# The low parts of the input weights made by an adding load instead of a VectorE subtraction, in a hybrid decoder step

## The chip, the cores and the metric

One core of a Trainium2 chip runs the kernel. The metric is the time of one execution on the device in microseconds (us), taken as the median of three runs; the profile is of one further execution. Engines are named as in the profile: PE is TensorE (PEld its weight loads), DVE is VectorE, ACT is ScalarE, POOL is GpSimd, SP is SyncE, which here only issues DMAs.

## What is computed

One inference step of a one-layer hybrid decoder, on a prompt of 512 tokens and 8 sample tokens, with model width 2048. A single input projection is split by columns into an mLSTM branch (4 heads of 256), a causal convolution branch (512 channels) and a sliding-window attention branch (8 query heads); their gated outputs are concatenated, multiplied by an output projection, and normalised with the residual. Cut to what matters here:

```python
h = jnp.einsum('btd,de->bte', x, w_in)            # the input projection, split by columns
...                                               # three branches, each with its gate
merged = jnp.concatenate([m_out, c_out * jax.nn.silu(cz), a_out * jax.nn.silu(az)], axis=-1)
y = jnp.einsum('bte,ed->btd', merged, w_out)
x = layer_norm(ALPHA * x + y, ln_g, ln_b)
```

Everything is float32.

## The kernel before, in words

The projections are float32 products made of three passes over parts of reduced precision. Each operand is taken apart into a high part (a rounding cast to float32r) and a low part (the operand less its high part). `mm3` (lines 209 to 212) then issues, for one 128 x 128 piece of weights, three matmuls into the same bank: line 210 takes the high weights and the high input, line 211 the **low weights** and the high input, line 212 the high weights and the low input. A transposed input of 520 columns is resident in 16 pieces (`xh`, `xl`), and is passed in two halves of 260 columns.

**The weight stream.** The list `stream` (lines 165 to 169) names all the weights in the order of their use, in tiles of 128 x 1024 float32 (512 KB). The input projection has NE = 62 column blocks of 128, called e, and each has two tiles, so tiles 0 to 123 are the input weights; tiles 124 and up belong to the output projection. `w_load` (line 180) issues a tile's load from HBM into a raw buffer `wr` on SP's queue; there are three raw buffers. `w_split` (line 187) takes the next tile from its raw buffer, takes a slot of `wh` (tag whi, 3 buffers) and of `wl` (tag wlo, 3 buffers), and calls `split` (lines 151 to 153):

```python
def split(hi, lo, raw):
    S.copy(out=hi, in_=raw)
    V.tensor_tensor(out=lo, in0=raw, in1=hi.bitcast(F32), op=ALU.subtract)
```

So ACT makes the high part (line 152) and DVE the low part (line 153), and after both the raw buffer is free for a later load.

**What sets the order.** The main loop over e (lines 994 to 1018) stands in a manual schedule for PE, DVE and ACT: these three engines run their instructions in the order of the program. POOL and SP are not in that list; the framework orders them. At the start of e, `w_split` is called for the first tile of e+1, and in its middle for the second one. The slots of that tile are those that the tile three places earlier used, and so the cast waits for PE to end with that tile. A tile is used by 16 calls of `mm3`, that is 48 matmuls on PE. After the matmuls of a half, the results are moved out of the bank (`post`, for the attention queries `post_aq`, lines 424 to 438), and `pump` lets the branches go on by some steps, each of which adds instructions to PE, ACT, DVE, and in the mLSTM and in the layer norms also to POOL: the mask addition (line 655), the product with the decay (line 686), and the power -0.5 of a variance (`rstd`, line 223). The sample attention (`att_sample`, line 526) copies queries into a padded tile with 32 small DVE instructions (line 548), which PE's line 555 reads. Before the loop come the first two column blocks with tiles 0 to 3, and the gate computation (`gates`, line 231), whose short ACT and DVE instructions run on into the loop's first 20 us.

Of the kernel before, what the change touches and what calls it, by code (L numbers as in the profile page):

```python
# [11 lines left out]
ALU = mybir.AluOpType  # L12
# [43 lines left out]
NE = len(ORDER)  # L56

TURNED = {(_i // 4, _i // 2 % 2, _i % 2): (_i - 1,) for _i in range(1, 9)}
TURNED.update({(3, 0, 1): (8, 9, 10, 11), (3, 1, 0): (12, 13, 14), (3, 1, 1): (15,)})
CONV0 = ORDER.index(("cg", 0))  # L60


# [11 lines left out]
def body(tc, ctx, A, O):  # L74
    nc = tc.nc
    V, S, G, PE, SP = nc.vector, nc.scalar, nc.gpsimd, nc.tensor, nc.sync
# [11 lines left out]
    def nm(s):  # L88
        uid[0] += 1
        return f"{s}{uid[0]}"  # L90
# [4 lines left out]
    def mid(dt=F32):  # L95
        return work.tile([P, 520], dt, tag="M", bufs=NM, name=nm("M"))
# [54 lines left out]
# [3 lines that stand above are left out]
# [3 lines left out]
    def x_tile(tag, dt=F32R):  # L157
        return res.tile([P, TT], dt, tag=tag, bufs=NK, name=nm(tag))
# [6 lines left out]
    stream = [A["w_in"][e, hf] for hf in range(2) for e in range(2)]  # L165
# [5 lines left out]
    raws, parts = {}, {}  # L171
# [8 lines left out]
    def w_load(n):  # L180
        while pos[0] < min(n, len(stream)):
            i = pos[0]
            raws[i] = wp.tile([P, 8 * P], F32, tag="wraw", bufs=NRAW, name=nm("wr"))
            SP.dma_start(out=raws[i], in_=stream[i])
            pos[0] += 1

    def w_split(n):
        while pos[1] < min(n, len(stream)):
            i = pos[1]
            w_load(i + 1)  # L190
            raw = raws.pop(i)
            if i in kept:

                if kept.index(i) < 2:
                    parts[i] = [[x_tile(t)[:, 0:512] for _ in range(2)] for t in ("xh", "xl")]
                else:
                    parts[i] = [[mid(F32R)[:, 0:512] for _ in range(2)] for _ in range(2)]
                for kk in range(2):
                    split(parts[i][0][kk], parts[i][1][kk], raw[:, kk * 512:(kk + 1) * 512])
            else:  # L200
                parts[i] = (wp.tile([P, 8 * P], F32R, tag="whi", bufs=3, name=nm("wh")),
                            wp.tile([P, 8 * P], F32R, tag="wlo", bufs=3, name=nm("wl")))
                split(*parts[i], raw)
                if i >= b2:
                    parts[i] = [[t[:, kk * 512:(kk + 1) * 512] for kk in range(2)] for t in parts[i]]
            pos[1] += 1
            w_load(i + 1 + ahead[0])
# [672 lines left out]
    for k in range(NK):  # L880
# [35 lines left out]
        if k == 5:  # L916
            w_split(3)
        if k == 8:
            w_split(4)
# [5 lines left out]
    for e in range(2):  # L925
        for k in range(NK - TAIL, NK):
            first(e, k)
        for hf in range(2):
            (post_ak, post_av)[e](ps01[e][hf], hf)
        w_split(5 + e)  # L930
# [17 lines left out]
    def before(name, i):  # L948

        if name == "mv" and i == 2:  # L950
            drain("att")
        elif name == "mq" and i == 6:
            drain(("m", 0))
        elif name == "cg" and i == 0:
            conv_state()
        elif name in ("mz", "mo"):
            drain(("m", i // 2))
        elif name == "cz":
            drain("conv")
# [33 lines left out]
    with tc.manual_schedule(engines=MAN):  # L993
        for e in range(2, NE):
            name, i = ORDER[e]
            w_split(2 * e + 3)
            budget = BUDGET if e < CONV0 else BUDGET2
            before(name, i)
# [295 lines left out]
```

## Time and profile before

| | |
|---|---|
| median of 3 runs | 1019.48 us (1019.22 to 1019.91) |
| the profiled execution | 1019.64 us |
| its span, first to last instruction | 1017.9 us |
| TensorE clock granted, mean over the span | 0.994 of full speed |
| PE busy | 997.0 us, 98% |
| DVE busy | 657.9 us, 65% |
| ACT busy | 396.6 us, 39% |
| POOL busy | 79.8 us, 8% |
| DMA | 147.11 MB, mean 145 GB/s |

How to read it: the profiled execution's time is 1.7 us above its span, and 0.16 us above the median of the runs. Issuing DMAs and waiting on semaphores are not counted as busy. PE's busy time is the union of overlapping matmuls, so that a share near 100% says that PE is seldom left without a matmul, and not that it runs at its peak.

### The profile page before, as it was taken

What the parts mean: (1) busy time and instruction counts of PE and PEld (TensorE: products, weight loads), DVE (VectorE), ACT (ScalarE), POOL (GpSimd) and SP (SyncE); (2) the same over time, 40 slices, a digit from 0 to 9 for tenths busy, and PEclk for the clock granted to TensorE, in tenths of its full rate; (3) what the DMA queues carried; (4) which work ended last, traced back from release to release, by engine and by line L of the source; (5) the groups of instructions that cost most, each with busy time, mean ns of one, the idle gap of its engine ahead of it and who ended that gap; (6) DMA issues with size and microseconds to landing.
All of it is one profiled execution on the core that took longest, in us unless ns stands there. A gap on an engine that the chain in (4) does not pass through costs nothing.

```text
span 1017.9 us, 19338 instructions
## 1 busy us (share of the span) xinstructions
PE 997.0 (98%) x7922; PEld 975.1 (96%) x7922; DVE 657.9 (65%) x1336; ACT 396.6 (39%) x713; POOL 79.8 (8%) x88
## 2 busy tenths in 40 slices
PE   8999999999999999999999999999999999999895
PEld 8999999899999999999999999999999999998675
DVE  4654667676646746756667777878654545559855
ACT  5553455234334433434442222222243433336341
POOL 1000000010101100001000000000000000005704
PEclk9999999999999999999999999999999999999998
DMA  8332213365445436635543232323234565555852
GB/s 275 130 105 76 71 63 106 120 211 189 135 166 183 153 117 211 190 106 169 180 153 103 100 93 101 88 89 104 96 120 141 186 228 173 175 171 189 264 169 83
DMA packets 64992, 147.11 MB, mean 145 GB/s; under 512 B 16181, under 2 KB 21261, under 8 KB 64904
## 3 DMA queue, kind: packets, MB, share of 16 engines
q1 hardware_dynamic: 64056, 143.64, 43.4%
q0 software_dynamic: 848, 2.25, 0.7%
q8 instruction: 62, 1.02, 0.4%
q14 instruction: 26, 0.21, 0.1%
HBM read 130.30 MB, written 15.56 MB: 143 GB/s over the span
## 4 chain that ended last, share of the span: by engine, by line
PE 86%; DVE 5%; DMA 4%; ACT 2%; issue 2%; POOL 0%; SPq 0%; DVEq 0%; ACTq 0%; POOLq 0%
PE mm L212 26%; PE mm L210 26%; PE mm L211 26%; DMA wr<-in_w_in 2%; DMA wr<-in_w_out 2%; PE bg L210 2%; PE bg L211 2%; PE bg L212 1%; DVE wl L153 1%; PE bg L677 1%; ACT wh L152 1%; PE bg L875 1%; PE bg L1077 1%; DMA S<-in_n 0%; DVE M L1047 0%
## 5 line engine op out<-in xcount | busy, mean ns | idle before, releaser
L210 PE MATMUL mm<-xh,wh 128*128 128x260 f32 (+1 forms) x2096 | 598.0, 285 | 2.8 <-ACT wh L152 1.6
L211 PE MATMUL mm<-xh,wl 128*128 128x260 f32 (+1 forms) x2096 | 592.3, 283 | 0.0
L212 PE MATMUL mm<-xl,wh 128*128 128x260 f32 (+1 forms) x2096 | 592.3, 283 | 0.0
L210 PEld LDWEIGHTS mm<-xh,wh 128*128 128x128 f32 x2096 | 396.0, 189 | 4.2 <-ACT wh L152 1.9
L211 PEld LDWEIGHTS mm<-xh,wl 128*128 128x128 f32 x2096 | 395.3, 189 | 0.6 <-DVE wl L153 0.2
L212 PEld LDWEIGHTS mm<-xl,wh 128*128 128x128 f32 x2096 | 394.6, 188 | 0.0
L153 DVE TENSOR_TENSOR wl<-wr,wh 128x1024 fp32r<-128x1024 f32 (+2 forms) x191 | 228.2, 1196 | 129.3 <-ACT wh L152 125.9
L152 ACT CAST wh<-wr 128x1024 fp32r<-128x1024 f32 (+2 forms) x191 | 193.9, 1016 | 220.8 <-PE mm L212 143.1
L341 DVE SCALAR_TENSOR_TENSOR L<-L,cst 128x512 f32<-128x512 f32 x120 | 90.0, 750 | 2.7
L811 ACT ACTIVATE S<-mm 128x260 f32<-128x260 f32 x48 | 18.7, 389 | 97.4 <-PE mm L212 97.4
L812 DVE TENSOR_TENSOR L<-L,S 128x260 f32<-128x260 f32 x48 | 20.6, 430 | 50.5 <-ACT S L811 50.5
L223 POOL TENSOR_TENSOR T<-T,mhalf 128x1 f32<-128x1 f32 (+1 forms) x26 | 16.3, 625 | 432.2 <-DVE T L221 403.9
L609 ACT ACTIVATE L<-mm 128x260 f32<-128x260 f32 x48 | 18.5, 385 | 64.7 <-PE mm L212 64.5
L784 DVE SCALAR_TENSOR_TENSOR M<-M,T,M 128x256 f32<-128x256 f32 x64 | 31.8, 496 | 10.9 <-ACT M L781 10.9
L212 PE MATMUL mm<-L,wh 128*128 128x264 f32 x128 | 36.4, 284 | 0.0
L211 PE MATMUL mm<-L,wl 128*128 128x264 f32 x128 | 36.4, 284 | 0.0
L210 PE MATMUL mm<-L,wh 128*128 128x264 f32 x128 | 36.3, 283 | 0.0
L787 DVE CUSTOM_DVE_ANT_0 S<-M,M 128x256 f32<-128x256 f32 x64 | 28.0, 438 | 2.2
L1048 POOL TENSOR_TENSOR M<-M,L 128x512 f32<-128x512 f32 (+1 forms) x12 | 25.7, 2156 | 2.6 <-PE bg L212 2.5
L211 PEld LDWEIGHTS mm<-L,wl 128*128 128x128 f32 x128 | 24.1, 188 | 0.0
L212 PEld LDWEIGHTS mm<-L,wh 128*128 128x128 f32 x128 | 24.1, 188 | 0.0
L210 PEld LDWEIGHTS mm<-L,wh 128*128 128x128 f32 x128 | 24.0, 188 | 0.0
(313 smaller groups left out, 1089.7 us busy)
## 6 DMA issues: line engine op xcount, KB each, us to landing
wr<-in_w_in SPq DMA_DIRECT2D x122, 512.0 KB
wr<-in_w_out SPq DMA_DIRECT2D x64, 512.0 KB
M<-in_C SPq DMA_DIRECT2D x32, 256.0 KB
M<-qkD SPq DMA_DIRECT2D x32, 256.0 KB
out_Cs<-M SPq DMA_DIRECT2D x32, 256.0 KB
M<-in_xT SPq DMA_DIRECT2D x15, 260.0 KB
M<-rowsD SPq DMA_DIRECT2D x8, 260.0 KB
M<-in_xp SPq DMA_DIRECT2D x8, 256.0 KB
```

Of the source, the lines that this page charges most:

```text
L152: S.copy(out=hi, in_=raw)
L153: V.tensor_tensor(out=lo, in0=raw, in1=hi.bitcast(F32), op=ALU.subtract)
L210: PE.matmul(out, lhsT=wh, rhs=h, start=start, stop=False)
L211: PE.matmul(out, lhsT=wl, rhs=h, start=False, stop=False)
L212: PE.matmul(out, lhsT=wh, rhs=l, start=False, stop=stop)
L341: V.scalar_tensor_tensor(out=y[:, 0:T], in0=t[:, k:k + T], scalar=cw[:, j, k:k + 1], in1=y[:, 0:T], op0=ALU.mult, op1=ALU.add)
L609: S.mul(out=hT[name, h][:, e, HS[hf]], in_=ps[:, 0:HALF], mul=1.0 / 16.0 if name == "mk" else 1.0)
L784: V.scalar_tensor_tensor(out=ce, in0=qkb[:, DK:2 * DK], scalar=gvv[:, e, b:b + 1], in1=ce, op0=ALU.mult, op1=ALU.add)
L787: V.tensor_tensor_reduce(out=junk, in0=ce, in1=qkb[:, 0:DK], scale=1.0, scalar=0.0, op0=ALU.mult, op1=ALU.add, accum_out=hc[:, e, b:b + 1])
L811: S.activation(out=s, in_=ps[:, 0:HALF], func=func)
L812: V.tensor_tensor(out=dst[:, HS[hf]], in0=dst[:, HS[hf]], in1=s, op=ALU.mult)
L1048: G.tensor_tensor(out=y, in0=y, in1=b, op=ALU.add)
```

## The change

For the tiles 8 to 123 of the stream the low part is no longer made by DVE. ACT makes the high part as before, and then, in a second instruction, writes the raw tile times -1 into the slot of the low part; that slot is of type float32r, so what is written is the negated high part. Then a DMA issued by POOL loads the same 512 KB of weights from HBM a second time, and adds them to what stands in the slot. The tiles 0 to 7, and those of the output projection, keep the subtraction.

```diff
 TURNED.update({(3, 0, 1): (8, 9, 10, 11), (3, 1, 0): (12, 13, 14), (3, 1, 1): (15,)})
+
+DMA0 = 8
 CONV0 = ORDER.index(("cg", 0))
...
                 parts[i] = (wp.tile([P, 8 * P], F32R, tag="whi", bufs=3, name=nm("wh")),
                             wp.tile([P, 8 * P], F32R, tag="wlo", bufs=3, name=nm("wl")))
-                split(*parts[i], raw)
+                if DMA0 <= i < 2 * NE:
+
+                    hi, lo = parts[i]
+                    S.copy(out=hi, in_=raw)
+                    S.mul(out=lo, in_=raw, mul=-1.0)
+                    G.dma_start(out=lo, in_=stream[i], accum_op=ALU.add)
+                else:
+                    split(*parts[i], raw)
```

## Rows read from the trace of the kernel before

**Rows 1.** The page, part 1: busy time, share of the span, instructions.

```profile
PE 997.0 (98%) x7922; PEld 975.1 (96%) x7922; DVE 657.9 (65%) x1336; ACT 396.6 (39%) x713; POOL 79.8 (8%) x88
```

**Rows 2.** Busy time by stretch: window, PE, PEld, DVE, ACT, POOL, clock, DMA share, GB/s.

```profile
60.00:184.00 124.00, 123.45 (x1015) 122.18 (x1013) 77.54 (x164) 57.27 (x144) 0.00 (x0) 1.00 0.25 83
184.00:240.00 56.00, 54.41 (x447) 53.42 (x448) 35.75 (x106) 20.32 (x43) 3.35 (x4) 1.00 0.62 199
...
400.00:500.00 100.00, 100.00 (x840) 99.71 (x840) 63.45 (x180) 43.27 (x78) 8.06 (x10) 1.00 0.53 167
...
600.00:710.00 110.00, 110.00 (x922) 110.00 (x922) 87.16 (x123) 27.53 (x39) 0.00 (x0) 1.00 0.31 96
...
sum 746.00, PE 743.86 PEld 740.26 DVE 486.08 ACT 274.72 POOL 31.20; mean PE 92.98 PEld 92.53 DVE 60.76 ACT 34.34 POOL 3.90
```

**Rows 3.** Waits of PE: who waited for whom, us in total, times, longest.

```profile
PE mm L212 <- DVE wl L153: 3.7, 3, 2.8
PE bg L555 <- DVE L L548: 1.8, 2, 0.9
```

**Rows 4.** Lines 152 and 153, the weight split: ns min/median/max, first and last start.

```profile
L152 ACT CAST wh<-wr x191: 297/1049/1072, 2.8 to 987.7; 128x1024 fp32r<-128x1024 f32 x182, 128x256 fp32r<-128x256 f32 x7, 128x128 fp32r<-128x128 f32 x2
L153 DVE TENSOR_TENSOR wl<-wr,wh x191: 286/1225/2364, 3.1 to 989.0; 128x1024 fp32r<-128x1024 f32 x182, 128x256 fp32r<-128x256 f32 x7, 128x128 fp32r<-128x128 f32 x2
```

**Rows 5.** Timeline around a tile's split and first use: start us, us, what.

```profile
641.29 1.05 ACT L152 CAST wh<-wr 128x1024 fp32r<-128x1024 f32 x1 [4.41 <-PE mm L212]
...
642.38 1.22 DVE L153 TENSOR_TENSOR wl<-wr,wh 128x1024 fp32r<-128x1024 f32 x1 [0.25 <-ACT wh L152]
...
652.69 0.28 PE L211 MATMUL mm<-xh,wl 128*128 128x260 f32 x1
```

**Rows 6.** The page, part 6: a store issued by POOL, KB, us to landing.

```profile
out_xp<-M POOLq DMA_DIRECT2D x8, 256.0 KB, 3.2
```

**Rows 7.** The page, part 3: SP's queue, packets, MB, share of 16 engines.

```profile
q1 hardware_dynamic: 64056, 143.64, 43.4%
```

**Rows 8.** Timeline around the split and first use of tile 8.

```profile
60.86 1.99 ACT L152 CAST wh<-wr 128x1024 fp32r<-128x1024 f32 x2
...
65.43 0.28 PE L211 MATMUL mm<-xh,wl 128*128 128x260 f32 x1
```

**Rows 9.** Timeline of PE: an idle time in the output projection.

```profile
947.56 0.50 PE L212 MATMUL mm<-wl,xh 128*128 128x512 f32 x1 [2.76 <-DVE wl L153]
```

**Rows 10.** Busy time by stretch, columns as in rows 2, just after rows 9.

```profile
948.00:950.00 2.00, 2.00 (x8) 1.57 (x7) 2.00 (x4) 0.89 (x1) 2.00 (x1) 0.64 0.75 184
950.00:952.00 2.00, 2.00 (x7) 1.54 (x6) 1.79 (x3) 0.85 (x2) 2.00 (x1) 0.51 0.69 207
```

**Rows 11.** Timeline around the split and first use of tile 50.

```profile
347.34 1.04 ACT L152 CAST wh<-wr 128x1024 fp32r<-128x1024 f32 x1
...
356.04 0.28 PE L211 MATMUL mm<-xh,wl 128*128 128x260 f32 x1
```

**Rows 12.** Timeline of ACT and DVE ahead of line 548's copies.

```profile
175.15 1.04 ACT L152 CAST wh<-wr 128x1024 fp32r<-128x1024 f32 x1
...
176.49 0.58 ACT L508 COPY M<-bg 64x512 f32<-64x512 f32 x1
...
176.83 1.22 DVE L153 TENSOR_TENSOR wl<-wr,wh 128x1024 fp32r<-128x1024 f32 x1
177.96 0.87 DVE L510 TENSOR_TENSOR L<-bg,M 64x128 f32<-64x128 f32 x4
```

**Rows 13.** POOL's DMA issues of line 1054: busy us, mean ns, idle before.

```profile
L1054 POOL DMA_DIRECT2D out_xp<-M x7 | 4.1, 583 | 0.9 <-POOL M L1048 0.6 <-DMA wr<-in_w_out 0.3
```

**Rows 14.** Waits of SP's queue: us in total, times, longest.

```profile
SPq L184 <- DVE wl L153: 522.2, 149, 10.8
```

**Rows 15.** Waits of POOL, and of DVE on POOL: us in total, times, longest.

```profile
POOL S L686 <- DVE T L787: 36.8, 5, 9.0
...
DVE T L623 <- POOL T L223: 10.5, 16, 0.7
```

## The prediction, as put on record before the run

> **What bounds the kernel now.** I read the page first: PE is busy for 98% of the span, DVE for 65%, ACT for 39% [rows 1]. Then the busy time by stretch, over the 746 us in which the input projection runs after the start-up and which hold all the tiles that change: PE has a matmul in flight for 743.86 of them, at the full granted clock [rows 2]. So this stage is bound by PE's own stream of matmuls, and all that a lighter DVE could give back there is the 2.1 us that are left. The waits of PE say who holds it up at all: the low parts made by DVE have ended three waits in the whole run, 3.7 us, and the longest, 2.76 us, lies in the output projection [rows 3, 9], whose tiles the change leaves alone. The next, 1.8 us, is for the sample attention's copies [rows 3]. DVE is thus no bound here, and the question is whether the new way of making the low part is in time.
>
> **How early the low part is now.** In the steady stage [rows 5] the cast of a tile starts as soon as its slot is free (641.29), DVE follows at 642.38 and ends 1.22 us later, and PE first reads the low part at 652.69. From the start of the cast to that matmul are 11.4 us, of which the split uses 2.3; 9.1 lie idle.
>
> **What goes.** The changed tiles are 2 x 62 - 8 = 116. DVE loses 116 subtractions of 1225 ns [rows 4], 142 us; all of them stood beside matmuls, so I count no gain. One place could give some: PE's wait for line 548. There a subtraction (176.83) stands directly in DVE's chain [rows 12]. But the new multiplication goes onto ACT right behind the cast of 175.15, and pushes line 508, now begun at 176.49, by some 1.05 us, so that it ends near 178.1; line 510 waits for it and started at 177.96. The late link moves from DVE to ACT, and I take 0 (ends: 0.9 us gained if ACT's order is kinder, 0.2 lost).
>
> **What is added on ACT.** 116 multiplications. None of this shape is in the trace; the cast of the same 128 x 1024 tile takes 1049 ns [rows 4], and I take that: 122 us on an engine that is busy for 275 of the 746 us [rows 2]. Its share rises from 37 to 53%, beside PE; ACT waits on PE, not PE on ACT, in the steady stage [rows 5], where the cast found ACT idle for 4.41 us. Where that cover is missing it costs one multiplication, 1.05 us, per wait; no wait of PE for an ACT evacuation is among its largest [rows 3], so 0. The raw buffer is released by ACT at cast + 2.1 us, where DVE did it at cast + 2.3. SP's queue, which waits for just that release before most weight loads [rows 14], gets it about as early, and what is queued behind it too: 0.
>
> **What is added on POOL and the DMA engines.** 116 issues on POOL. The issues in the trace take 583 ns [rows 13], so 68 us on an engine that has 31 us of work in the stage [rows 2]: hidden, unless the order is bad (rival below). And 116 more reads of 512 KB. SP's queue moved 143.64 MB in 43.4% of 16 engines' span [rows 7], that is 325 GB/s while busy, so 512 KB (0.52 MB) are 1.6 us of all engines; 116 of them are 187 us, which raises the DMA share of the stage from a mean of about 0.40 to 0.65.
>
> **How late the low part becomes.** The trace has no adding load. The nearest row is a plain store of 256 KB from POOL's queue: 3.2 us from issue to landing [rows 6]. Another 256 KB at 325 GB/s are 0.8, so 4.0 us if adding costs nothing. If the tile that is added to must be read as well, that is 512 KB more, 1.6 us: 5.6. If a raw load shares the engines all the time, another 1.6: 7.2. I take 5.6, since what is added to must come from somewhere, and the share in the quiet stretches (0.25 and 0.31 [rows 2]) leaves most of the time free; 4.0 and 7.2 are the ends. The Trainium skill, Collectives: The Full Stack, section The bandwidth ceiling, says that an add in the DMA path reads two sources through one ring and so runs at half the rate of a copy; no run here shows it. By that rule the load is at 5.6 us rather than 4.0, and the sum 1024.5 rather than 1021.2.
>
> With 5.6 the low part lands at cast + 2.1 (two ACT instructions) + 0.1 (the hand-over) + 5.6 = 7.8 us, against 11.4 in the steady stage [rows 5]: hidden by 3.6 us, and by 2.0 with 7.2.
>
> **The sum.** Two kinds of tile have less.
>
> - *Tile 8, the first that changes.* Its cast starts only at 60.86, because ACT is still at the gates' instructions, and two casts take 1.99 us [rows 8]. The first ends near 61.9; the multiplication brings it to 62.95, the hand-over to 63.05. PE reads the low part at 65.43 [rows 8]. That leaves 2.4 us, and 5.6 overrun it by **3.2 us** (ends 1.6 and 4.8). Nothing covers this: PE takes its matmuls in order. DVE met it, with 1.2 us of work after the cast.
> - *The clock after such a wait.* PE's one wait of 2.76 us [rows 9] is followed by a stretch at 0.64 and 0.51 of the clock [rows 10]; 0.5 is the level 1.2 GHz, and the two rows are 1.4 and 2.0 us at it, some 1.7 us lost. The idle 1.6 us spread in 184 to 240 brought no fall (1.00 [rows 2]). At 3.2 us I take the fall: **1.7 us** (ends 0 and 1.7).
> - *Tight tiles.* In 200 to 525 us some casts come late because ACT is at mLSTM work. The tightest is tile 50: cast at 347.34, low part read at 356.04 [rows 11], which leaves 6.5 us for the load; I count ten such tiles, up to 7.4 us. With 5.6 they hold: **0**. With 7.2 four of them are short by 0.55 to 0.75, 2.6 us in all.
>
> Sum: 1019.64 + 3.2 + 1.7 = 1024.5 us against the profiled execution's own time, which is 0.16 above the median shown; too little to shift the number. With the lower ends 1021.2, with the upper ones 1028.7.
>
> **The rivals.**
>
> - *Not slower.* The load at tile 8 is quick. The point is 2.4 + 2.0 = 4.4 us from issue to landing: below it the wait is under 2 us, the clock stays up, and the time is 1019.6 to 1021.5. For it: 4.0 is the plain sum, and nothing but tile 8 is tight. Against: tile 11's and 12's raw loads start in that very time, since two raw buffers come free.
> - *POOL's order.* An adding load is issued in POOL's order, which the program does not fix. If it lands behind a product of line 686 that waits for DVE, up to 9.0 us and 36.8 in five waits [rows 15], or if the powers stand behind loads, it is late by the wait. A wait of 7.4 us on top of 5.6 overruns the steady 9.1 by 3.9; five of them are 19 us, with the forecast's 4.9 some 1044. For it: POOL has 31 us of such work in the stage [rows 2], and DVE waits for it 16 times [rows 15]. Against: in program order these operations precede the split on DVE as well, and DVE's subtraction had to wait for the same things.
> - *The DMA engines become the bound.* At twice the bytes, 3.2 us per add, the 15.5 adds of each 100 us take 0.50 of the engines, and 400 to 500 already has 0.53 [rows 2]: just full. Over the whole stage the point is 0.60 x 746 / 116 = 3.9 us of all engines per add; beyond it PE starves throughout. At 4.8 us the load is 0.40 + 0.75 = 1.15, and 746 us become 858: about 1130. For it: nothing shows the price of an add. Against: it needs more than twice a copy.
> - *Faster.* All 2.1 us of PE's idle time in the stage go, and tile 8 is in time: 1017.5. It needs the subtraction at 176.83 to be the true link, and a load under 2.4 us where the store of half the bytes took 3.2 [rows 6].
>
> That the change does nothing of what it says would read as the first rival: DVE would keep its 658 us.
>
> **How the numbers follow.** A measurement of this kernel can tell 0.2%, 2.0 us, from no change: faster is below 1017.4, slower above 1021.5. Forecast (1021.2 to 1028.7) 0.52, not slower 0.20, POOL's order 0.12, DMA bound 0.12, faster 0.04. Slower is then 0.52 + 0.12 + 0.12 = 0.76, the same 0.20, faster 0.04. A range from 1019.8 to 1048 holds the forecast, POOL's order, most of the case of no change, and the mild beginning of the DMA bound, together 0.8; the rest of the DMA bound and the gain are left out.
>
> **What would show it.** Right: DVE's busy time falls by about 142 us and ACT's rises by about 122; PE's waits have a new one on the adding load near 65 us, of about 3 us, with a clock below 1.00 behind it; after that the busy time of PE by stretch stays near full to 800 us; the issue of POOL has a landing near 5.6 us. Wrong: a landing under 4.4 us (no wait worth the name), or over 9.1 (a wait at nearly every tile); waits of PE for the load only between 200 and 550 us, where POOL computes, would speak for its order; a DMA share near 1 in 400 to 500 for the engines.

## The result, and the profile after

| | before | after |
|---|---|---|
| median time, us | 1019.35 (1018.79 to 1019.91) | 1073.74 (1073.45 to 1074.16) |
| ratio, 95% interval | | 1.0536 [1.0523, 1.0548] |
| profiled execution, us | 1019.64 | 1073.45 |
| its span, us | 1017.9 | 1071.6 |
| granted clock of its span, mean | 0.994 | 0.977 |

Both medians are of four runs. The changed kernel is slower by 54.4 us. "Slower" was right; the time lies far above the predicted 1024.5 and beyond the range's end of 1048. In the code after, the multiplication is line 209 and the adding load line 210; the high part's cast of a changed tile is line 208; split's cast and subtraction are now lines 154 and 155; the three matmuls of a projection chunk are lines 219 to 221 (before: 210 to 212); the raw load is line 186, and the lines of the branches stand 9 further down.

Part 1 of the page answers to [rows 1]:

```profile
PE 1010.1 (94%) x7922; PEld 984.4 (92%) x7922; DVE 522.5 (49%) x1220; ACT 505.8 (47%) x829; POOL 177.3 (17%) x204
```

DVE is relieved of 135.4 us, ACT has 109.2 more, and PE, with the same 7922 matmuls, is busy for 13.1 us longer. The rest of the 53.7 us of span is PE's idle time: 1071.6 - 1010.1 = 61.5 us, where before it was 1017.9 - 997.0 = 20.9, so 40.6 more. The first lines of PE's waits (us in total, times, longest) say for whom:

```profile
PE mm L220 <- DMA wl<-in_w_in: 27.8, 16, 7.1
PE bg L598 <- ACT M L593: 11.6, 1, 11.6
```

Neither has a like among PE's waits before. The first is the adding load, late 16 times. The second is one wait of the sample attention, which the change doesn't touch. Together they are 39.4 of the 40.6 us.

Busy time by stretch, columns as in [rows 2], says where:

```profile
60.00:184.00 124.00, 115.03 (x922) 112.86 (x921) 48.81 (x112) 66.21 (x143) 14.75 (x17) 0.97 0.64 146
184.00:240.00 56.00, 42.55 (x324) 41.27 (x323) 18.85 (x81) 21.08 (x43) 7.18 (x8) 0.88 0.66 162
240.00:300.00 60.00, 56.01 (x465) 55.59 (x464) 28.80 (x103) 32.78 (x56) 12.17 (x15) 0.98 0.88 243
300.00:400.00 100.00, 94.87 (x766) 94.36 (x765) 38.18 (x139) 45.90 (x80) 17.46 (x22) 0.96 0.85 224
400.00:500.00 100.00, 100.00 (x841) 99.66 (x840) 42.70 (x159) 52.06 (x88) 19.14 (x25) 1.00 0.92 226
500.00:600.00 100.00, 95.02 (x776) 93.90 (x775) 47.85 (x157) 50.90 (x80) 19.11 (x23) 0.98 0.87 215
600.00:710.00 110.00, 106.04 (x868) 105.25 (x867) 60.19 (x97) 43.76 (x57) 15.57 (x18) 0.98 0.83 180
```

The DMA share (the last column but one) has risen from 0.25 to 0.64 at the start and from 0.31 to 0.83 at the end. Yet the stretch with the highest, 400 to 500 with 0.92, is the one in which PE has no gap at all. The lost time lies in single waits, and the longer ones bring a lower clock with them (0.88 in 184 to 240, where the wait of line 598 is).

The load itself stands in part 5 (busy, mean ns of one, idle before), part 6 (KB, median us to landing) and part 3 (packets, MB, share of 16 engines) of the page:

```profile
L210 POOL DMA_DIRECT2D wl<-in_w_in x116 | 100.9, 869 | 572.9 <-ACT wl L209 491.7
...
wl<-in_w_in POOLq DMA_DIRECT2D x116, 512.0 KB, 8.1
...
q1 hardware_dynamic: 64056, 143.64, 42.7%
q0 software_dynamic: 17552, 63.07, 32.1%
```

It lands 8.1 us after its issue, not 5.6, and 8.1 is beyond the upper end of 7.2. POOL before an issue waits for ACT's multiplication, 491.7 of 572.9 us: POOL is mostly idle when the multiplication ends. POOL's DMA queue takes 32.1% of 16 engines' span; what stands on it before and in e1, mostly the output's stores, takes 0.7%, so the adds take 31.4% x 1071.6 / 116 = 2.9 us of all engines each.

Tile 8 is the longest of the 16 waits. The timelines of ACT, POOL and PE around it (start, us, what; in brackets the idle time before), and then busy time by stretch behind it, columns as above:

```profile
61.06 1.06 ACT L209 ACTIVATE wl<-wr 128x1024 fp32r<-128x1024 f32 x1
...
62.43 0.94 POOL L210 DMA_DIRECT2D wl<-in_w_in  x1 [48.19 <-ACT wl L209]
...
71.93 0.59 PE L220 MATMUL mm<-xh,wl 128*128 128x260 f32 x1 [7.09 <-DMA wl<-in_w_in]
```

```profile
72.00:74.00 2.00, 2.00 (x9) 2.00 (x10) 0.00 (x0) 0.00 (x0) 0.00 (x0) 0.50 1.03 303
74.00:76.00 2.00, 2.00 (x12) 2.00 (x11) 0.00 (x0) 0.00 (x0) 0.00 (x0) 0.52 1.05 236
76.00:78.00 2.00, 2.00 (x19) 2.00 (x19) 0.00 (x0) 0.00 (x0) 0.00 (x0) 1.00 0.28 57
```

The multiplication ends at 62.12, POOL issues 0.3 us later (0.1 was foreseen), and the tile is there 9.5 us after the issue: PE stands for 7.09 us, and then works until 76 at half its clock (0.50 and 0.52, the level of 1.2 GHz; 9 and 12 matmuls where the next 2 us have 19): some 4 us at half, 2.0 lost. The DMA engines are full until 76 (1.03, 1.05) and at 0.28 after it: the raw loads of the next tiles and the adding load of tile 9 go at the same time.

### The profile page after: what moved, and what is told of

It is laid out like the page before. It is cut to its first block, busy times and chain, and to the rows that moved or that the text cites. A ratio compares the mean times of both kernels' runs of the same rounds, so it can differ in the third digit from the quotient of the medians.

```text
span 1071.6 us, 19498 instructions
## 1 busy us (share of the span) xinstructions
PE 1010.1 (94%) x7922; PEld 984.4 (92%) x7922; DVE 522.5 (49%) x1220; ACT 505.8 (47%) x829; POOL 177.3 (17%) x204
## 3 DMA queue, kind: packets, MB, share of 16 engines
q0 software_dynamic: 17552, 63.07, 32.1%
## 4 chain that ended last, share of the span: by engine, by line
PE 69%; DMA 18%; issue 5%; DVE 3%; ACT 3%; POOL 1%; SPq 0%; POOLq 0%; DVEq 0%; ACTq 0%
PE mm L220 21%; PE mm L221 20%; PE mm L219 20%; DMA wl<-in_w_in 12%; DMA wr<-in_w_in 3%; DMA M<-rowsD 2%; PE bg L219 1%; PE bg L221 1%; PE bg L220 1%; DVE wl L155 1%; DMA wr<-in_w_out 1%; ACT wh L208 1%; ACT wl L209 1%; PE bg L884 1%; DVE M L1056 1%
## 5 line engine op out<-in xcount | busy, mean ns | idle before, releaser
L220 PE MATMUL mm<-xh,wl 128*128 128x260 f32 (+1 forms) x2096 | 598.4, 285 | 27.8 <-DMA wl<-in_w_in 27.8
L220 PEld LDWEIGHTS mm<-xh,wl 128*128 128x128 f32 x2096 | 399.6, 191 | 31.9 <-DMA wl<-in_w_in 31.4
L221 PEld LDWEIGHTS mm<-xl,wh 128*128 128x128 f32 x2096 | 399.1, 190 | 0.0
L210 POOL DMA_DIRECT2D wl<-in_w_in x116 | 100.9, 869 | 572.9 <-ACT wl L209 491.7
L208 ACT CAST wh<-wr 128x1024 fp32r<-128x1024 f32 x116 | 121.4, 1047 | 133.7 <-issue 112.9
L209 ACT ACTIVATE wl<-wr 128x1024 fp32r<-128x1024 f32 x116 | 122.8, 1059 | 0.0
L155 DVE TENSOR_TENSOR wl<-wr,wh 128x1024 fp32r<-128x1024 f32 (+2 forms) x75 | 86.6, 1156 | 55.5 <-ACT wh L154 53.5
L154 ACT CAST wh<-wr 128x1024 fp32r<-128x1024 f32 (+2 forms) x75 | 72.6, 970 | 63.9 <-PE mm L221 27.6
L716 DVE SCALAR_TENSOR_TENSOR M<-M,M,bg 128x258 f32<-128x258 f32 x24 | 10.5, 480 | 48.8 <-PE bg L221 48.8
```

What stands on the lines that cost most here:

```text
L209: S.mul(out=lo, in_=raw, mul=-1.0)
L210: G.dma_start(out=lo, in_=stream[i], accum_op=ALU.add)
L220: PE.matmul(out, lhsT=wl, rhs=h, start=False, stop=False)
L221: PE.matmul(out, lhsT=wh, rhs=l, start=False, stop=stop)
```

## Experiments

The theory after this result: the adding load is slow because the multiplication that triggers it also frees the raw buffer, so that SP's next raw load starts with it; what is then late costs PE directly at some tiles, and through SP's queue at line 598. Rivals: ACT's extra instruction; the engines' throughput; the order on POOL. Each edit is to the changed kernel, and each ratio is to runs of the kernel before beside it.

### e1: no adding load

```
-                    G.dma_start(out=lo, in_=stream[i], accum_op=ALU.add)
```

> The adding load is left out, ACT's multiplication stays: the low part of tiles 8 to 123 is the negated high part, nothing is loaded a second time. Theory (the landing of the adding load ends PE's waits): no wait for a low part is left, 1018 to 1021 us, clock mean 0.99. Rival (ACT, with one more instruction of 1.06 us per tile, holds up its evacuations and casts): 1045 us or more, with PE waiting for ACT.

Measured: 1018.66 us, ratio 0.9991 [0.9982, 1.0001]. PE's waits begin:

```profile
PE mm L220 <- DVE wl L155: 2.9, 2, 2.3
PE mm L218 <- ACT wh L154: 2.0, 2, 1.8
```

ACT's 116 multiplications, DVE's 116 subtractions fewer and the earlier or later release of the raw buffers are worth nothing that can be told from zero. The whole loss is the load's. It is also the floor for any version of this change: an add that came for free would be no faster than the kernel before.

### e2: a plain load in place of the adding one

```
-                    G.dma_start(out=lo, in_=stream[i], accum_op=ALU.add)
+                    G.dma_start(out=lo, in_=stream[i])
```

> The second load stays on POOL's queue with the same bytes and the same waits, but it overwrites the slot in place of adding (the low part of tiles 8 to 123 is then the whole weight). Theory (an added packet takes 0.328 us of an engine where a copied one takes 0.159, so the load is in flight twice as long): packets near 0.16 us, landing 5 to 6.5 us in place of 8.1, 1022 to 1032 us. Rival (any second load from POOL's queue beside the raw load lands as late, whatever it does): landing near 8, 1065 to 1075 us.

Measured: 1029.31 us, ratio 1.0107 [1.0089, 1.0126], +9.8. From part 3 of the page, and from PE's waits:

```profile
q0 software_dynamic: 17552, 63.07, 17.8%
```

```profile
PE bg L598 <- ACT M L593: 5.1, 1, 5.1
...
PE mm L220 <- DMA wl<-in_w_in: 2.6, 2, 2.1
```

With the same packets and the same bytes on the queue, a plain load takes (17.8 - 0.7)% x 1027.5 / 116 = 1.5 us of all engines, the adding one 2.9: twice. On this the rule that the prediction cited (the Trainium skill, Collectives: The Full Stack, section The bandwidth ceiling, half the rate for an add) and the trace agree. The time and the landing (5.0 us over all tiles) are in the range expected. Of the 54.4 us, some 10 come from 116 more loads of any kind, and 44 from their being adds.

The landing of line 210 in the quiet stretch from 620 to 700, first after, then e2:

```profile
DMA to landing us min/median/max: 7.4/7.9/11.0
```

```profile
DMA to landing us min/median/max: 4.2/4.4/8.1
```

Adding costs 3.5 us of landing there. A maximum of 11.0 stands against a margin of 11.4 - 2.1 - 0.1 = 9.2 us [rows 5], so even steady tiles are overrun now and then (tile 96 has the 11.0).

### e3 and e4: move the raw load away from the add

e3 adds from the raw tile, which is in SBUF already, so the raw buffer is held until the add has landed. e4 puts the raw loads of the changed tiles on POOL's queue, where they stand in one line with the adds.

```
-                    G.dma_start(out=lo, in_=stream[i], accum_op=ALU.add)
+                    G.dma_start(out=lo, in_=raw, accum_op=ALU.add)
```

```
-            SP.dma_start(out=raws[i], in_=stream[i])
+            (G if 11 <= i < 2 * NE else SP).dma_start(out=raws[i], in_=stream[i])
```

> The adding load reads the raw tile in SBUF in place of HBM, and so holds the raw buffer until it lands. Theory (the adding load is late since a raw load, released at the same moment, shares the engines with it): the raw load now starts after the landing, landing near 5.3 us, packets still near 0.33, 1021 to 1032 us. Rival (the engines' total busy time decides, 2.9 us per add): time as with the change, 1065 us or more. Rival (raw loads now start 5 us later and become late): waits of ACT for raw loads, 1040 or more.

> The raw loads of tiles 11 to 123 are issued by POOL too, behind the adding load in one queue, in place of SP's. Theory (the two loads share the engines packet by packet when they stand in two queues): in one queue the add goes first, landing 5.3 to 6 us; and raw loads no longer stand behind the small stores of the sample attention, so the wait of 11.6 us at line 598 goes: 1021 to 1035 us. Rival (order of the queues is of no matter): 1060 us or more. Rival (POOL's order delays raw loads): ACT waits for raw loads, over 1040.

Measured: e3 1061.25 us, ratio 1.0428 [1.0396, 1.0461], +41.7; e4 1043.53 us, ratio 1.0240 [1.0225, 1.0255], +24.0. Both are above what was expected (at most 1032 and 1035 us). The same landing row from 620 to 700, e3 and e4:

```profile
DMA to landing us min/median/max: 4.9/6.2/7.9
```

```profile
DMA to landing us min/median/max: 5.0/6.2/7.4
```

Both bring 6.2 us, against 7.9. The timelines of SP's queue and of POOL after show the meeting, on one tile:

```profile
642.56 0.33 SPq L186 DMA_DIRECT2D wr<-in_w_in  x1
```

```profile
642.83 0.86 POOL L210 DMA_DIRECT2D wl<-in_w_in  x1 [5.10 <-ACT wl L209]
```

Raw load and add start 0.27 us apart, because the same multiplication releases both; at 101 of the 116 tiles they start within half a microsecond of each other. The 6.2 us are not yet the add alone. In e3 the landing of one tile frees the raw buffer, and the load so started meets half of the 14 adds from 620 to 700: seven where it starts 0.9 us or more behind the add land in 4.9 to 6.0 us, the seven where it starts earlier in 6.3 to 7.9. So the add alone takes some 5.5 us, and some 2 of the 7.9 us are the raw load beside it. But the time follows the landing only in part. The waits of PE, e3 and then e4:

```profile
PE mm L220 <- DMA wl<-in_w_in: 4.6, 5, 2.8
```

```profile
PE mm L220 <- DMA wl<-wr: 15.3, 11, 4.5
PE bg L598 <- ACT M L593: 12.2, 1, 12.2
```

In e4 (the first fence) the waits for the add shrink from 27.8 to 4.6 us, and line 598's is gone. In e3 (the second) 15.3 are left. Its raw buffers are held longer, so that, as I read it, the raw loads and with them the casts come later: four of its eleven late tiles (37, 44, 50, 69; 7.6 of the 15.3 us) have only 0.3 to 5.1 us left for the landing, where before they had 6.5 to 7.2. Line 598's wait stays in e3, as the raw loads are still on SP's queue. What is left in e4 is again a wait that the change doesn't touch. PE's longest, and POOL's instruction behind it:

```profile
PE bg L219 <- ACT S L154: 9.3, 1, 9.3
```

```profile
223.40 1.26 POOL L664 TENSOR_TENSOR M<-M,mmask 128x512 f32<-128x512 f32 x1 [19.01 <-DMA M<-rowsD]
```

POOL stands 19.01 us for the load of M from rowsD, ACT stands for POOL, and PE for ACT. The load was issued late. From SP's queue in e4:

```profile
203.41 14.06 SPq L757 DMA_DIRECT2D T<-rowsD  x1
...
218.06 0.42 SPq L661 DMA_DIRECT2D M<-rowsD  x1
```

The queue stands 14.06 us in an issue ahead of it, which comes right behind the stores of the sample's caches, those that e7 below leaves out. One load that is issued late on SP's queue costs PE twice as much waiting as all late adds of e4 together. e4 without these stores was not run.

### e5: the change from tile 9 on

```
-DMA0 = 8
+DMA0 = 9
```

> Tile 8 keeps VectorE's subtraction, the tiles 9 to 123 are made by the adding load. Theory (each late tile costs its wait and, where the clock falls behind it, half of the stretch at half the clock): the wait of 7.1 us at tile 8 goes, and 6.8 us at half the clock behind it, 3.4 us; tile 9 may be late by 1 to 2 us in its place: 1062 to 1066 us. Rival (PE makes the lost time good later, where it waits for something else): 1070 us or more.

Measured: 1064.57 us, ratio 1.0441 [1.0411, 1.0471], +45.3, so 9.1 less than with tile 8. PE's waits:

```profile
PE mm L220 <- DMA wl<-in_w_in: 22.5, 19, 5.4
```

The time given back agrees with what tile 8 shows in the trace after, 7.1 us of wait and 2.0 of half clock, but the interval of e5 alone is some 3 us to either side. The waits' row has only 5.3 us fewer, with 19 smaller waits in place of 16; but it is of an execution of 1068.55 us, the longest of e5's (1060.86 to 1068.55), so where the late tiles lie differs from one execution to the next. Tile 8 is about a sixth of the loss, and not, as forecast, all of it.

### e6, e7, e8: the late tiles, the caches' stores, both

e6 makes the low parts of 16 tiles, the ones PE waited for, by DVE's subtraction as before. e7 leaves out the two big stores of the sample's key and value caches. e8 does both.

```
+LATE = (8, 12, 16, 19, 22, 37, 50, 68, 69, 72, 75, 80, 95, 96, 103, 117)
...
-                if DMA0 <= i < 2 * NE:
+                if DMA0 <= i < 2 * NE and i not in LATE:
```

```
-    SP.dma_start(out=O["ks"], in_=kc[:, :, 1:129])
-    SP.dma_start(out=O["vs"][0:P - 1], in_=vc[1:P])
```

> The 16 tiles whose low part PE waited for (8, 12, 16, 19, 22, 37, 50, 68, 69, 72, 75, 80, 95, 96, 103, 117) keep VectorE's subtraction, the other 100 are made by the adding load. Theory (the landing against the time left): 27.8 us of waits and some 10 us of clock go, the wait at line 598 stays: 1033 to 1042 us. Rival (the adds load the DMA engines everywhere, and other tiles become late in their place): over 1050 us.

> The changed kernel without the two stores of the sample's key and value caches (lines 544 and 549: the outputs new_k_s and new_v_s stay unwritten but for their newest row), which are 512-byte packets on SP's queue. Theory (the raw load behind them is late since the adds now take turns with them): the wait of 11.6 us at line 598 goes and half of some 6 us at half the clock: 1056 to 1062 us. Rival (that wait comes from ScalarE's order or from an adding load): unchanged, 1070 us or more.

> Both edits: the 16 late tiles on VectorE, and the two stores of the caches left out. Theory (three causes hold all of the loss: late landings, the raw load behind the small stores, the clock behind long waits): 1019 to 1027 us. If something else took part of the 54 us: over 1035 us.

| kernel | median, us | ratio, 95% interval | to before, us | to after, us |
|---|---|---|---|---|
| e6 | 1040.62 | 1.0214 [1.0192, 1.0236] | +21.4 | -33.0 |
| e7 | 1059.24 | 1.0391 [1.0376, 1.0407] | +40.0 | -14.4 |
| e8 | 1027.45 | 1.0072 [1.0052, 1.0092] | +8.2 | -46.2 |

The waits of PE, first e6 (one line further down by its own edit, as in e8), then e7, then e8:

```profile
PE bg L599 <- ACT M L594: 10.4, 1, 10.4
...
PE mm L221 <- DMA wl<-in_w_in: 1.8, 3, 0.8
```

```profile
PE mm L220 <- DMA wl<-in_w_in: 27.7, 16, 6.9
```

```profile
PE mm L221 <- DMA wl<-in_w_in: 5.4, 5, 1.4
```

Each removes its own wait and leaves the other's: the two causes are separate, 33.0 + 14.4 = 47.4 against 46.2 together. e6 and e7 are in the range expected, e8 half a microsecond above it. What e8 still loses, 8.2 us, is partly 5.4 us at five other tiles, which 100 adding loads still make late; the rest I have not traced.

How the sample attention's wait comes about, in the changed kernel (SP's queue, then ACT, then PE), and the same cast before:

```profile
189.18 0.27 SPq L549 DMA_DIRECT2D out_vs<-L  x1
189.54 13.86 SPq L186 DMA_DIRECT2D wr<-in_w_in  x1
```

```profile
220.88 1.04 ACT L208 CAST wh<-wr 128x1024 fp32r<-128x1024 f32 x1 [15.01 <-DMA wr<-in_w_in]
221.83 1.05 ACT L209 ACTIVATE wl<-wr 128x1024 fp32r<-128x1024 f32 x1
222.79 0.57 ACT L593 COPY M<-bg 128x512 f32<-128x512 f32 x1
```

```profile
198.64 1.05 ACT L152 CAST wh<-wr 128x1024 fp32r<-128x1024 f32 x1 [4.40 <-DMA wr<-in_w_in]
```

A raw load stands on SP's queue right behind a cache's store, and its issue takes 13.86 us. Its tile is late; ACT, which takes its work in order, stands 15.01 us in front of the tile's cast, and line 593's copy, which PE's line 598 needs, is queued behind that cast. Before, the same cast waited 4.40 us, and PE never noticed. The DMA engines are not full meanwhile. Busy time by stretch, columns as in [rows 2], while PE stands after, and at the same place before:

```profile
216.00:218.00 2.00, 0.00 (x0) 0.00 (x0) 0.00 (x0) 0.00 (x0) 0.00 (x0) 0.50 0.06 27
```

```profile
192.00:194.00 2.00, 2.00 (x19) 2.00 (x18) 1.07 (x5) 0.15 (x1) 0.00 (x0) 1.00 0.06 27
```

A DMA share of 0.06 is one engine of 16. As I read it, one engine works off line 549's store by itself, and the raw load behind it can't land before. (That store is of 127 rows of 4 KB, and not, as expected for e7, of 512-byte packets: of the 1168 packets that e7 takes off SP's queue only 1041 are under 2 KB.) Three adds are issued in that time (188.80, 192.13 and 202.89); at 2.9 us of every engine each they hold that one up by some 8.7 us, an estimate, and the cast's wait has grown by 10.6. The two stores were not left out one by one, so that it is line 549's is not shown by a run. Both sides are needed: without the stores (e7) the wait is gone, without the adds it is 0.6 us (e1), and with plain loads 5.1 (e2).

## Why the prediction was wrong in size, point by point

The direction was right for a reason that holds for about a sixth of the loss, tile 8. The rest came in through two terms that the sum had at 0: the raw load beside the add, and what is queued behind on SP.

- **DVE no bound, ACT's multiplication 0, DVE's relief 0: right**, by e1. DVE's fall (135.4 against 142) and ACT's rise (109.2 against 122) were near.
- **Tile 8 first and longest, the clock falls behind it: right in kind.** 3.2 + 1.7 us forecast; 7.1 + 2.0 measured, and 9.1 us of time by e5. The clock's term held; the wait's failed with the landing, 9.5 us at this tile. The two raw loads beside it stand in the prediction, under the rival "not slower", without a price.
- **The landing, 5.6 (4.0 to 7.2): the term that was mis-sized.** With no raw load beside the add 5.6 is right. At six of the ten tight tiles SP's queue starts none from 6 us before the add until 1.6 us or more after it, and they land in 5.3 to 5.8 us (tile 29, in the stretch of line 598's wait, is like them and takes 7.1). Tile 44, issued at 340.96, its landing and SP's next raw load:

```profile
DMA to landing us min/median/max: 5.3/5.3/5.3
```

```profile
342.53 0.43 SPq L186 DMA_DIRECT2D wr<-in_w_in  x1
```

  With the raw load beside it, 7.9 in the quiet stretch, and a median of 8.2 at the 101 tiles where both start together. The upper end had the raw load as 1.6 us, and it measured some 2; but what failed is that the forecast left it out, since "the share in the quiet stretches (0.25 and 0.31 [rows 2]) leaves most of the time free". That share was read as if the add met raw loads by chance, but the change itself makes both start at one moment. The choice should have been 7.2, with an upper end above 8.
- **Tight tiles, 0: wrong**, though not because all ten were late. PE waited at four of them (37, 50, 69 and 75). The other six are those with no raw load beside the add, and were in time. The 27.8 us of waits are tile 8 with 7.1, the four with 12.4, four tiles between 60 and 184 us that the forecast didn't count as tight (12, 16, 19 and 22, with 7.4 to 7.7 us of room before) with 1.9, and seven with 8.6 to 9.8 us of room before with 6.4. (The prediction's price for 7.2, 2.6 us, is 2.3 by the rooms in the trace before.) The largest of the four, tiles 50 and 37, were late by their casts, which "what is queued behind it too: 0" denied: their room shrank from 6.5 and 6.7 us to 2.9 and 3.4, and even 5.6 us would not have met it. At tile 50, POOL, then ACT:

```profile
381.01 1.28 POOL L664 TENSOR_TENSOR M<-M,mmask 128x512 f32<-128x512 f32 x1 [9.64 <-DMA M<-rowsD]
```

```profile
383.02 0.41 ACT L154 CAST S<-S 128x256 fp32r<-128x256 f32 x1 [4.53 <-POOL S L695]
383.34 1.04 ACT L208 CAST wh<-wr 128x1024 fp32r<-128x1024 f32 x1
```

  POOL's mask waits 9.64 us for a load of M, ACT 4.53 us for POOL, and tile 50's cast stands behind that; PE then waits 5.13 us for its add. Tile 37 has the same chain and waits 3.56. This step, **what is queued behind on SP: 0**, is the second that failed, and the one that no size of the landing mends: I looked at when SP's queue is released, and not at what the other transfers on the engines do when the adds take 2.9 us of all 16 for each tile. Line 598's wait, 14.4 us of the time by e7, is the same mistake.
- **Rival, POOL's order: fell.** POOL waits for ACT, and 111 of the 116 issues follow the multiplication by 0.3 to 0.4 us; of the other five the latest comes 4.45 us behind it, and PE waited at none of them. An issue takes 869 ns, not 583.
- **Rival, the DMA engines the bound: fell as told.** 2.9 us per add lies under its point of 3.9, and PE is full at a share of 0.92. The outcome lies between this rival and the forecast: lateness well before the engines are full.
- **Clock.** 13.1 of the 53.7 us are PE's own, matmuls that run at half clock behind the longer waits. In the forecast that was one stretch; with the waits of line 598 and of other tiles it became several. e8, without these waits, has PE busy for nearly the time of before (part 1 of its page):

```profile
PE 997.8 (97%) x7922; PEld 974.0 (95%) x7922; DVE 538.6 (52%) x1236; ACT 490.5 (48%) x813; POOL 165.3 (16%) x188
```

## What to carry to other kernels

When work moves from an engine to the DMA queues, ask what the same release starts besides the new transfer, and price the two together; a mean share of the engines says nothing about two transfers with one trigger. Then list the transfers that hold a queue for long, the loads that are queued behind them, and the engines that take their work in order and wait for those: here one late raw load, which the sum had at 0, cost 14.4 us, about three times the 4.9 that were counted. Relief on an engine that ends no wait is worth nothing: here 135 us of it moved the time by less than could be measured.

## What the runs showed that was not expected

Adding from an SBUF tile takes the engines no less time than adding from HBM: in e3 POOL's queue has 31.9% of a span of 1057.2 us, which with the stores' 0.7% off is 2.8 us of all engines per add, against 2.9. Part 3 of e3's page:

```profile
q0 software_dynamic: 17552, 63.07, 31.9%
```

And an issue on POOL is longer for the adding load than for the store it was priced by, 869 ns against 583; the plain load of e2, with the same bytes, takes 530.
